# Norm2 between the first products of two pairs, two operand sets in the down-projection, and the gate row moved behind the sum

## Chip, cores and metric

The kernel runs on one core of one Trainium2 chip. The metric is the device time of one execution in microseconds (us), taken as the median of several runs.

## What is computed

One layer of a hybrid decoder, in float32: 1024 positions, model width 1024, and a gated MLP with 2816 channels in each half. The first sub-layer (attention and a state-space branch, with its output projection) is the first half of the kernel, and the change leaves it alone except for two buffers. What the change touches is the second sub-layer:

```python
h = _modulate(_rmsnorm(x, norm2_g[l]), sh2, sc2)          # norm2
up = _causal_dwconv(h @ ffn_w_up[l], ffn_conv_w[l], ffn_conv_b[l])
val, gate = jnp.split(up, 2, axis=-1)
x = x + g2[:, None, :] * ((jax.nn.gelu(gate) * val) @ ffn_w_down[l])
```

Here g2 is a row of 1024 gates, one for each output column. It is itself a product of the condition vector with a weight matrix, computed in the kernel.

## The kernel before

**Products.** Every float32 product is made of three matmuls of a reduced type: each operand is split into a high part (a copy, made on ScalarE, ACT) and a low part (a subtraction, made on VectorE, DVE), and hi·hi, hi·lo and lo·hi are summed in PSUM. A product of one 128-channel operand with a 512-deep, 512-wide block of the normalised input takes 12 such matmuls (lines 982 to 984).

**Up-projection.** The 2816 channels of each half are 22 pairs m of tiles (a value tile and its gate tile). For a pair the weights are a 2x2 block matrix A11, A12, A21, A22, and the normalised input is a 2x2 block matrix B11, B12, B21, B22; B11 and B21 come from the late half of the positions, the others from the early half. From pair 2 on the four block products of a pair are made by seven products in place of eight (Strassen-Winograd): the sums S1 to S4 of the weight blocks are made on GpSimd (POOL), and the sums T1 to T4 of the input blocks on DVE, once, in norm2. The seven products of a pair are A11·B11, A12·B21, S2·T2, S1·T1, S3·T3, S4·B22 and A22·T4. Pair 0 is made by eight products without S sums (A11, A12, A21, A22 with B11 and B21, then with T1, the early half's first block, and B22). Pair 1 is made by seven, with its first two products ahead. `up_raw` loads a weight block, `up_split` splits it, `up_early` does both, `up_operands` makes the operands of a pair with its sums, `product` issues the 12 matmuls, `conv` makes the convolution, the gelu and the gating of a pair and stores it to `a_d`.

**Norm2.** It is made by quarters g of the positions, in the order 3, 2, 1, 0. `norm2_x` scales the rows, `norm2_t` transposes them on TensorE (PE; `tp`, line 938), modulates them on ACT (`h2f`, line 939) and splits them. The quarters 3 and 2 give B11 and B21. The quarters 1 and 0 give T1 and B22, and `norm2_s` and `norm2_4` then give T2, T3 and T4: this is a chain of 128x512 operations that go back and forth between ACT and DVE.

**Down-projection.** The 1024 output columns are two halves n, the positions are eight tiles t, each with its own PSUM bank. `down_operands` loads 128 channels of the gated activations (`araw`) and of w_down (`wdraw`), multiplies the latter by the gate row g2row on POOL (line 1160), and splits both. `down` issues three matmuls for each t (lines 1174 to 1176). The last three m of each half are done tile by tile, and the tile's sum is added to the stored x (line 1189) and written out.

**What sets the order.** The program is written in the Tile framework. Its scheduler decides the order of instructions on each engine ahead of the run, from its own simulation; on the chip each engine takes its instructions strictly in that order. Buffers come from pools, and an instruction that reuses a buffer waits for the last reader. SyncE (SP) issues the loads and stores in order too: a transfer that has to wait for its buffer holds up all those behind it.

Of the kernel before, what the change touches and what calls it, by code (L numbers as in the profile page):

```python
# [9 lines left out]
F32 = mybir.dt.float32  # L10
F32R = mybir.dt.float32r
# [11 lines left out]
NT = 8  # L23
# [12 lines left out]
def hybrid_layer_kernel(  # L36
# [85 lines left out]

    A1 = const.tile([128, 8], F32, name="A1")
# [3 lines left out]
    g1row = const.tile([128, 1024], F32, name="g1row")  # L127
# [661 lines left out]
    def ssm_stats(inv):  # L789
        after_v(lambda: sp.dma_start(out=oS, in_=o_d.rearrange("(k p) j c -> p k j c", p=128)))  # L790
        yield
        yield from mix_scale(osp, psB_new("nps"), oS, range(NT), True, inv)
        yield
# [43 lines left out]
    def tail_stats(g):  # L837
        inv = small.tile([128, 2], F32, tag="ainv", name="ainv", bufs=4)
        run_all(mix_scale(osp, psB_new("nps"), oT, (2 * g, 2 * g + 1), False, inv))
        tail.append((g, inv))  # L840
        if len(tail) > 1 and g > 0:
            tail_proj()
# [51 lines left out]
    RAWS, OPS = 6, 7  # L894
# [117 lines left out]
    ups = [new_up() for _ in range(2)]  # L1012
    up = ups[0]
    a, b, c = new_bank(0, "a", "V", "a", 2), new_bank(0, "b", "V", "b"), new_bank(0, "c", "V", "a", 2)
    product(a, 0, "A11", B11, True, True)
    act_copy(up[0][:, LATE], a)
    product(b, 0, "A12", B21, True, True)
    tt(dve, up[0][:, LATE], b, up[0][:, LATE], ADD)
    product(c, 0, "A21", B11, True, True)
    act_copy(up[1][:, LATE], c)  # L1020
    d = new_bank(0, "d", "N", "b")
    product(d, 0, "A22", B21, True, True)
    tt(dve, up[1][:, LATE], d, up[1][:, LATE], ADD)
    product(new_bank(1, "a", "N", "c"), 1, "A11", B11, True)
    product(new_bank(1, "b", "V", "b"), 1, "A12", B21, True)

    norm2_t(1, norm2_x(1))
    norm2_s(1)
    with tc.high_priority():
        xn0 = norm2_x(0)  # L1030
# [5 lines left out]
    norm2_t(0, xn0)  # L1036
    psT.release()
    pools["D"] = alloc("psD", bufs=1, space=PSUM)
    product(a, 0, "A11", T1, False)
    product(c, 0, "A21", T1, False)  # L1040
    norm2_s(0)
    product(a, 0, "A12", B22, False)
    act_copy(up[0][:, EARL], a)
    product(c, 0, "A22", B22, False)
    act_copy(up[1][:, EARL], c)
    norm2_4(0)
    qp.release()
    uc = alloc("ffnconv", side="right")
    g2row = g1row
# [18 lines left out]
    def up_operands(m):  # L1068

        for r in range(2):  # L1070
            for c in range(2):
                if (m, r, c) not in raws:
                    up_raw(m, r, c)
        q11, q12, q21, q22 = [raws[m, r, c] for r in range(2) for c in range(2)]
        s1, s2, s3, s4 = [us.tile([128, 4, 128], F32, tag="S", name="S", bufs=4) for _ in range(4)]
        if m > 1:
            up_split(m, "A11", q11)
        tt(pool, s1, q21, q22, ADD)
        tt(pool, s2, s1, q11, SUB)
        if m > 1:  # L1080
            up_split(m, "A12", q12)
# [21 lines left out]
    def up_pair(m):  # L1103
        up_operands(m)
        up = ups[m] if m < 2 else new_up()
        if m > 1:
            a = new_bank(m, "a", "V", "a", 2)
            product(a, m, "A11", B11, True)
        a = bank[m, "a"]
        act_copy(up[0][:, LATE], a)  # L1110
        if m > 1:
            product(new_bank(m, "b", "NV"[m % 2], "b"), m, "A12", B21, True)
        b = bank[m, "b"]
# [14 lines left out]
    conv(0, ups[0])  # L1128
    for m in range(1, NM):
        up_pair(m)  # L1130
        if 6 <= m < 10:
            g2_rows(m - 6)
# [10 lines left out]
    us.release()  # L1143
    xq.release()
    da = alloc("dact")
    dw = alloc("dwgt")
# [3 lines left out]
    def down_operands(m, n):  # L1150
        raw = da.tile([128, 1024], F32, tag="araw", name="araw", bufs=2)
        sp.dma_start(out=raw, in_=a_d[m * 128:(m + 1) * 128, :])
        hi = da.tile([128, 1024], F32R, tag="ahi", name="ahi", bufs=4)
        lo = da.tile([128, 1024], F32R, tag="alo", name="alo", bufs=4)
        act_copy(hi, raw)
        tt(dve, lo, raw, hi.bitcast(F32), SUB)
        ns = slice(n * 512, (n + 1) * 512)
# [3 lines left out]
        whi = dw.tile([128, 512], F32R, tag="wdhi", name="wdhi", bufs=4)  # L1161
        wlo = dw.tile([128, 512], F32R, tag="wdlo", name="wdlo", bufs=4)
# [5 lines left out]
    for n in range(2):  # L1168
# [9 lines left out]
        for m in range(NM - TAIL):  # L1178
            ops = down_operands(m, n)
            for t in range(NT):  # L1180
                down(t, m, ops)
        ops = [down_operands(m, n) for m in range(NM - TAIL, NM)]
        for t in range(NT):
# [5 lines left out]
            tt(dve, res, o[t], res, ADD)  # L1189
# [4 lines left out]
    dw.release()  # L1194
    da.release()
# [63 lines left out]
```

## Time and profile before

| | us |
|---|---|
| median of 3 runs (1341.87 to 1342.91) | 1342.84 |
| the profiled execution | 1337.98 |
| its span in the trace | 1336.2 |
| TensorE busy in the span | 1211.5 (91%) |
| VectorE busy | 1019.7 (76%) |
| ScalarE busy | 594.0 (44%) |
| GpSimd busy | 535.4 (40%) |

All positions in time below are microseconds from the start of the span of this one profiled execution. The second sub-layer's matmuls begin at about 630 us, the down-projection at 1091 us. A bracket at the end of a row of a timeline gives the idle time of the engine ahead of the instruction and what ended it. "Clk" is the TensorE clock that was granted in a stretch, as a share of full speed.

### The profile page before, as it was taken

The page shows a single profiled execution, that of the slowest core. Times are in us where ns is not written, and L with a number is a line of the kernel's source. Part 1 is how long each engine was busy: PE and PEld are TensorE (multiplying, and loading weights), DVE is VectorE, ACT ScalarE, POOL GpSimd, SP SyncE. Part 2 cuts the span into 40 slices and gives each one's busy share as a digit, 9 for nine tenths or more (in the row PEclk, how much of TensorE's full clock was granted, in tenths as well). Part 3 has the DMA queues.
Part 4 walks back from the last instruction along what each step waited for, and adds up shares of the span by engine and source line. Part 5 has one row for each costly group of instructions (what it writes and reads, how often), then busy time and mean ns, then how long its engine had stood idle before and what let it go on. Part 6 is the DMA issues. An engine that isn't in the chain of part 4 may idle for free.

```text
span 1336.2 us, 16685 instructions
## 1 busy us (share of the span) xinstructions
PE 1211.5 (91%) x5740; PEld 989.2 (74%) x5740; DVE 1019.7 (76%) x1531; ACT 594.0 (44%) x1006; POOL 535.4 (40%) x415
## 2 busy tenths in 40 slices
PE   5879989999769988679788999999999989999998
PEld 4667768777557776568567888788888878888887
DVE  6999988973887999996799678877777666554552
ACT  5431333331565676535554554445554543222320
POOL 4472451431762446810253553454435334222330
PEclk9989979989679999889889999999999999999999
DMA  8462445557943755041024223322222145447543
GB/s 342 159 143 55 131 136 148 152 152 241 252 111 99 215 175 173 16 142 79 17 87 134 81 88 102 103 95 79 79 93 81 56 157 196 145 145 239 174 142 111
DMA packets 125632, 177.83 MB, mean 133 GB/s; under 512 B 36454, under 2 KB 73958, under 8 KB 124524
## 3 DMA queue, kind: packets, MB, share of 16 engines
q1 hardware_dynamic: 105484, 156.85, 37.7%
q10 hardware_dynamic: 20064, 19.93, 4.5%
q8 instruction: 45, 0.74, 0.2%
q14 instruction: 39, 0.32, 0.1%
HBM read 134.67 MB, written 40.89 MB: 131 GB/s over the span
## 4 chain that ended last, share of the span: by engine, by line
PE 54%; DVE 28%; DMA 8%; issue 4%; ACT 3%; POOL 1%; SPq 1%; DVEq 0%; ACTq 0%; POOLq 0%
PE dnps L1175 6%; PE dnps L1176 6%; PE dnps L1174 6%; PE up_a L982 5%; PE up_a L984 5%; PE up_a L983 5%; DVE ada_acc L67 4%; DVE nb L703 3%; DMA ada_raw<-in_ada_r_dram 3%; PE up_c L982 2%; PE up_c L984 2%; PE up_c L983 2%; PE wops L776 2%; PE wops L777 2%; PE wops L778 2%
## 5 line engine op out<-in xcount | busy, mean ns | idle before, releaser
L61 POOL TENSOR_TENSOR S<-upraw 128x512 f32<-128x512 f32 x42 | 83.4, 1987 | 253.3 <-DVE uplo L61 173.2
L1175 PE MATMUL dnps<-wdlo,ahi 128*128 128x512 f32 x352 | 137.2, 390 | 0.8 <-DVE wdlo L61 0.8
L1174 PE MATMUL dnps<-wdhi,ahi 128*128 128x512 f32 x352 | 134.6, 390 | 3.4 <-ACT wdhi L160 3.4
L1176 PE MATMUL dnps<-wdhi,alo 128*128 128x512 f32 x352 | 137.1, 390 | 0.0
L61 DVE TENSOR_TENSOR uplo<-S,uphi 128x512 fp32r<-128x512 f32 x84 | 96.4, 1151 | 45.4 <-ACT uphi L160 44.2
L61 DVE TENSOR_TENSOR alo<-araw,ahi 128x1024 fp32r<-128x1024 f32 x44 | 61.9, 1407 | 87.7 <-ACT ahi L160 87.7
L61 POOL TENSOR_TENSOR sig<-sig,nb 128x127 f32<-128x127 f32 (+3 forms) x64 | 94.2, 1479 | 84.2 <-DVE nb L703 58.2
L67 DVE SCALAR_TENSOR_TENSOR cv<-up,cols_sb,cv 128x1023 f32<-128x1023 f32 x88 | 116.2, 1322 | 14.3 <-ACT cv L1095 13.2
L61 POOL TENSOR_TENSOR wdraw<-wdraw,g1row 128x512 f32<-128x512 f32 x44 | 69.4, 1581 | 140.7 <-DMA wdraw<-in_w_down_dram 136.3
L703 DVE TENSOR_TENSOR_SCAN nb<-nb 128x128 f32<-128x128 f32 (+3 forms) x64 | 108.4, 1708 | 2.3 <-ACT nb L701 2.0
L160 ACT ACTIVATE ahi<-araw 128x1024 fp32r<-128x1024 f32 x44 | 46.6, 1060 | 141.8 <-PE dnps L1175 119.3
L160 ACT ACTIVATE uphi<-S 128x512 fp32r<-128x512 f32 x84 | 52.7, 631 | 103.6 <-PE up_c L983 30.9
L67 DVE SCALAR_TENSOR_TENSOR ada_acc<-ada_raw,c_sb,ada_acc 128x256 f32<-128x256 f32 (+1 forms) x97 | 73.4, 771 | 25.6 <-DMA ada_raw<-in_ada_r_dram 23.7
L553 PE MATMUL qkvp<-w_hi,hhi 128*128 128x512 f32 x192 | 78.8, 412 | 3.8 <-DVE qssq L606 2.9
L554 PE MATMUL qkvp<-w_lo,hhi 128*128 128x512 f32 x192 | 78.4, 408 | 0.8 <-POOL w_lo L61 0.8
L1174 PEld LDWEIGHTS dnps<-wdhi,ahi 128*128 128x128 f32 x352 | 66.0, 188 | 17.6 <-ACT wdhi L160 3.8
L555 PE MATMUL qkvp<-w_hi,hlo 128*128 128x512 f32 x192 | 77.4, 403 | 0.0
L1175 PEld LDWEIGHTS dnps<-wdlo,ahi 128*128 128x128 f32 x352 | 66.1, 188 | 14.9 <-DVE wdlo L61 1.2
L1176 PEld LDWEIGHTS dnps<-wdhi,alo 128*128 128x128 f32 x352 | 66.1, 188 | 13.5
L160 ACT ACTIVATE uphi<-upraw 128x512 fp32r<-128x512 f32 x67 | 41.8, 629 | 64.5 <-PE up_a L983 26.7
L61 POOL TENSOR_TENSOR cv<-cv 128x1024 f32<-128x1024 f32 x22 | 54.5, 2475 | 34.6 <-ACT cv L1099 34.5
L1095 ACT ACTIVATE cv<-up,cols_sb 128x1024 f32<-128x1024 f32 x44 | 54.7, 1244 | 24.5 <-DVE up L61 23.8
(328 smaller groups left out, 3515.5 us busy)
## 6 DMA issues: line engine op xcount, KB each, us to landing
upraw<-in_w_up_dram SPq DMA_DIRECT2D x88, 256.0 KB, 2.6
araw<-a_d SPq DMA_DIRECT2D x44, 512.0 KB, 3.3
ada_raw<-in_ada_r_dram SPq DMA_DIRECT2D x48, 256.0 KB, 3.1
a_d<-cv ACTq DMA_DIRECT2D x22, 512.0 KB, 2.7
wdraw<-in_w_down_dram SPq DMA_DIRECT2D x44, 256.0 KB, 3.3
ada_raw<-in_ada_a_dram SPq DMA_DIRECT2D x8, 1024.0 KB, 9.4
qk_d<-hl ACTq DMA_DIRECT2D x32, 256.0 KB, 3.0
q<-qk_d SPq DMA_DIRECT2D x32, 256.0 KB, 6.0
```

The lines of the kernel that those rows point to most:

```text
L61: eng.tensor_tensor(out=out, in0=a, in1=b, op=op)
L67: dve.scalar_tensor_tensor(out=out, in0=a, scalar=s, in1=b, op0=op0, op1=op1)
L160: act.activation(out=o, in_=i, func=AF.Copy)
L553: pe.matmul(o, lhsT=lh, rhs=his[k], start=(k == 0), stop=False)
L554: pe.matmul(o, lhsT=lh, rhs=los[k], start=False, stop=False)
L703: dve.tensor_tensor_scan(out=nb[:, 0:n][:, ::-1], data0=nb[:, 0:n][:, ::-1], data1=nb[:, 0:n][:, ::-1], initial=1.0, op0=MUL, op1=ALU.bypass)
L982: pe.matmul(ps, lhsT=hi[:, kt, :], rhs=rh, start=(first and kt == 0), stop=False, skip_group_check=True)
L983: pe.matmul(ps, lhsT=hi[:, kt, :], rhs=rl, start=False, stop=False, skip_group_check=True)
L984: pe.matmul(ps, lhsT=lo[:, kt, :], rhs=rh, start=False, stop=(kt == 3), skip_group_check=True)
L1174: pe.matmul(o[t], lhsT=hi[:, a], rhs=whi, start=(m == 0), stop=False)
L1175: pe.matmul(o[t], lhsT=hi[:, a], rhs=wlo, start=False, stop=False)
L1176: pe.matmul(o[t], lhsT=lo[:, a], rhs=whi, start=False, stop=(m == NM - 1))
```

## The change

Norm2's quarters 1 and 0 are moved between the first products of the pairs 0 and 1, and both pairs are made by eight products: pair 1's S sums go, and one product is added. The raw weight buffers are 4 and 2 in place of 6 common ones, the operand sets 8 in place of 7. The x tile's pool and the S pool stay allocated to the end, and the down-projection gets two separate sets of operand buffers, one of them in the room of B11 and B21. The multiplication by the gate row goes from w_down (POOL) to the finished sum (DVE, one more 128x512 operation for each of the 16 output tiles). The core of the diff:

```diff
@@ -891,13 +891,16 @@
-    RAWS, OPS = 6, 7
+    OPS, FIRST = 8, 2
...
-        raw = fu.tile([128, 4, 128], F32, tag="upraw", name="upraw", bufs=RAWS)
+        if m >= FIRST and r == 1:
+            raw = uc.tile([128, 4, 128], F32, tag="upraw", name="upraw", bufs=2)
+        else:
+            raw = fu.tile([128, 4, 128], F32, tag="upraw", name="upraw", bufs=4)
@@ -1009,23 +1012,36 @@
...
+    def first_late(m, pa, pb, pc, pd):
+        up = ups[m]
+        a = new_bank(m, "a", *pa)
+        product(a, m, "A11", B11, True, True)
+        act_copy(up[0][:, LATE], a)
+        b = new_bank(m, "b", *pb)
+        product(b, m, "A12", B21, True, True)
+        tt(dve, up[0][:, LATE], b, up[0][:, LATE], ADD)
...
+    def first_early(m):
+        up, a, c = ups[m], bank[m, "a"], bank[m, "c"]
+        product(a, m, "A11", T1, False)
+        product(c, m, "A21", T1, False)
+        product(a, m, "A12", B22, False)
+        act_copy(up[0][:, EARL], a)
+        product(c, m, "A22", B22, False)
+        act_copy(up[1][:, EARL], c)
 
     norm2_t(1, norm2_x(1))
+    first_late(0, ("V", "a", 2), ("V", "b"), ("V", "a", 2), ("N", "b"))
     norm2_s(1)
+    up_early(1, ("A21", "A22"))
     with tc.high_priority():
         xn0 = norm2_x(0)
@@ -1034,19 +1050,16 @@
     norm2_4(1)
     norm2_t(0, xn0)
+    first_late(1, ("N", "c"), ("V", "b"), ("N", "b"), ("V", "b"))
...
+    first_early(0)
     norm2_s(0)
...
+    first_early(1)
     norm2_4(0)
...
@@ -1140,26 +1149,23 @@
...
-    us.release()
-    xq.release()
-    da = alloc("dact")
-    dw = alloc("dwgt")
+
+    dps = [alloc(f"dops{i}") for i in range(2)]
...
-        raw = dw.tile([128, 512], F32, tag="wdraw", name="wdraw", bufs=3)
-        sp.dma_start(out=raw, in_=w_down[m * 128:(m + 1) * 128, ns])
-        tt(pool, raw, raw, g2row[:, ns], MUL)
...
+        raw = dp.tile([128, 512], F32, tag="wdraw", name="wdraw", bufs=2)
+        sp.dma_start(out=raw, in_=w_down[m * 128:(m + 1) * 128, n * 512:(n + 1) * 512])
...
+            with tc.high_priority() if (m, n) == (0, 0) else ExitStack():
+                ops = down_operands(m, n)
...
-            tt(dve, res, o[t], res, ADD)
+            t_ = dx.tile([128, 512], F32, tag="tmp", name="tmp", bufs=2)
+            tt(dve, t_, o[t], g2row[:, ns], MUL)
+            tt(dve, res, t_, res, ADD)
```

In SP's order, the loads of the first weight blocks (`upraw`) stood ahead of most of the stores of x (`x_d`). Before:

```order
L901 DMA upraw<-in_w_up_dram 128x512 x6
L852 DMA x_d<-xs 128x1024
L901 DMA upraw<-in_w_up_dram 128x512 x4
L852 DMA x_d<-xs 128x1024 x3
L852 DMA x_d<-xq_5302 128x1024 x2
L852 DMA x_d<-xq_5303 128x1024 x2
L901 DMA upraw<-in_w_up_dram 128x512 x2
```

The same place after the change:

```order
L852 DMA x_d<-xs 128x1024 x4
L904 DMA upraw<-in_w_up_dram 128x512 x6
L852 DMA x_d<-xq_5302 128x1024
L904 DMA upraw<-in_w_up_dram 128x512 x4
L852 DMA x_d<-xq_5302 128x1024
L904 DMA upraw<-in_w_up_dram 128x512 x2
L852 DMA x_d<-xq_5303 128x1024 x2
L904 DMA upraw<-in_w_up_dram 128x512 x2
```

The four stores from `xs` now stand ahead of all six loads, and the stores from `xq` stand between further loads.

On PE, the end of norm2, with the last transposes (`tp`) and the first products with T1 of pair 0 (up_a and up_c are the banks of a pair). Before:

```order
L938 MATMUL tp_6339<-ident,xn 128x128 x2
L938 MATMUL tp_6291<-ident,xn 128x128 x2
L938 MATMUL tp_6298<-ident,xn 128x128 x2
L938 MATMUL tp_6346<-ident,xn 128x128 x2
L938 MATMUL tp_6361<-ident,xn 128x128 x2
L938 MATMUL tp_6339<-ident,xn 128x128 x2
L938 MATMUL tp_6346<-ident,xn 128x128 x2
L938 MATMUL tp_6368<-ident,xn 128x128 x2
L938 MATMUL tp_6361<-ident,xn 128x128 x2
L938 MATMUL tp_6368<-ident,xn 128x128 x2
L982 MATMUL up_a<-T1hi_6158,uphi 128x512
L982 MATMUL up_c<-T1hi_6158,uphi 128x512
```

The same place after the change:

```order
L985 MATMUL up_d<-B21hi_5848,uphi 128x512
L986 MATMUL up_d<-B21lo_5850,uphi 128x512
L987 MATMUL up_d<-B21hi_5848,uplo 128x512
L985 MATMUL up_d<-B21hi_5848,uphi 128x512
L941 MATMUL tp_6347<-ident,xn 128x128 x2
L986 MATMUL up_d<-B21lo_5850,uphi 128x512
L987 MATMUL up_d<-B21hi_5848,uplo 128x512
L941 MATMUL tp_6354<-ident,xn 128x128 x2
L941 MATMUL tp_6347<-ident,xn 128x128 x2
L941 MATMUL tp_6354<-ident,xn 128x128 x2
L985 MATMUL up_a<-T1hi_6158,uphi 128x512
L985 MATMUL up_c<-T1hi_6158,uphi 128x512
```

Before, the last 22 transposes stood in a row behind the last product of the late half. Now the last of them stand between the matmuls of pair 1's product with B21 (up_d).

On ACT, the change from the up-projection to the down-projection (`ahi` and `wdhi` are the first operands of the latter, `cv` is the convolution). Before:

```order
L1095 ACTIVATE cv<-up,cols_sb 128x1024
L160 ACTIVATE up<-up_a 128x512
L1095 ACTIVATE cv<-up,cols_sb 128x1024
L160 ACTIVATE ahi<-araw 128x1024
L160 ACTIVATE wdhi<-wdraw 128x512
L1099 ACTIVATE cv<-cv 128x1024
L160 ACTIVATE ahi<-araw 128x1024
```

The same place after the change:

```order
L160 ACTIVATE up<-up_a 128x512
L1106 ACTIVATE cv<-up,cols_sb 128x1024
L160 ACTIVATE ahi<-araw 128x1024
L160 ACTIVATE up<-up_a 128x512
L160 ACTIVATE wdhi<-wdraw 128x512 x2
L160 ACTIVATE up<-up_a 128x512
L1106 ACTIVATE cv<-up,cols_sb 128x1024
L160 ACTIVATE ahi<-araw 128x1024
```

The first `ahi` and `wdhi` stood behind the last convolution of pair 21 (the second `cv<-up`, row before them); now they stand ahead of the evictions and the convolution of pair 21.

## Rows read from the trace of the kernel before

**Rows 1.** Page: busy us per engine; chain; a costly group; a DMA group.

```profile
PE 1211.5 (91%) x5740; PEld 989.2 (74%) x5740; DVE 1019.7 (76%) x1531; ACT 594.0 (44%) x1006; POOL 535.4 (40%) x415
...
PE 54%; DVE 28%; DMA 8%; issue 4%; ACT 3%; POOL 1%; SPq 1%; DVEq 0%; ACTq 0%; POOLq 0%
...
L61 POOL TENSOR_TENSOR wdraw<-wdraw,g1row 128x512 f32<-128x512 f32 x44 | 69.4, 1581 | 140.7 <-DMA wdraw<-in_w_down_dram 136.3
...
upraw<-in_w_up_dram SPq DMA_DIRECT2D x88, 256.0 KB, 2.6
```

**Rows 2.** Waits of PE, 630 to 700: us in total, times, longest.

```profile
PE tp L938 <- ACT h2f L939: 8.0, 5, 3.4
PE up_a L982 <- ACT uphi L160: 5.6, 1, 5.6
```

**Rows 3.** Stretches: length, then busy us (instructions) per engine, clk, DMA share, GB/s.

```profile
651.00:677.00 26.00, 12.15 (x36) 7.62 (x37) 22.85 (x37) 14.86 (x30) 13.54 (x3) 0.67 0.00 0
...
724.00:730.00 6.00, 5.93 (x19) 4.72 (x20) 4.37 (x9) 1.99 (x4) 1.40 (x1) 0.72 0.59 197
...
1100.00:1300.00 200.00, 200.00 (x884) 165.70 (x883) 107.04 (x86) 60.33 (x77) 62.50 (x39) 1.00 0.54 177
```

**Rows 4.** Timeline of PE, 646 to 666: start, duration, instruction, idle before.

```profile
646.75 0.82 PE L938 MATMUL tp<-ident,xn 128*128 128x128 f32 x6
647.33 0.47 PE L982 MATMUL up_b<-B21hi,uphi 128*128 128x512 f32 x1
...
665.16 0.63 PE L984 MATMUL up_a<-T1hi,uplo 128*128 128x512 f32 x1
665.58 0.63 PE L982 MATMUL up_a<-T1hi,uphi 128*128 128x512 f32 x1
```

**Rows 5.** Timeline of DVE, 640 to 676.

```profile
639.43 0.75 DVE L924 TENSOR_SCALAR xn<-xq,n2inv 128x1024 f32<-128x1024 f32 x1
...
648.04 0.69 DVE L61 TENSOR_TENSOR mix<-h2f,B11hi 128x512 f32<-128x512 f32 x1 [2.83 <-ACT h2f L939]
...
663.81 0.69 DVE L61 TENSOR_TENSOR T1lo<-mix,T1hi 128x512 fp32r<-128x512 f32 x1
...
669.83 0.70 DVE L61 TENSOR_TENSOR mix<-mix,B21lo 128x512 f32<-128x512 f32 x1
...
675.49 1.78 DVE L61 TENSOR_TENSOR T1lo<-mix,T1hi 128x512 fp32r<-128x512 f32 x1
```

**Rows 6.** Timeline of ACT, 672 to 676.

```profile
673.02 1.15 ACT L160 ACTIVATE uphi<-S 128x512 fp32r<-128x512 f32 x2 [6.97 <-POOL S L61]
674.08 0.62 ACT L160 ACTIVATE T1hi<-mix 128x512 fp32r<-128x512 f32 x1
```

**Rows 7.** Timeline of POOL, 640 to 676.

```profile
660.97 10.67 POOL L61 TENSOR_TENSOR S<-upraw 128x512 f32<-128x512 f32 x1 [79.98 <-DVE T L61]
671.72 1.26 POOL L61 TENSOR_TENSOR S<-S,upraw 128x512 f32<-128x512 f32 x1
```

**Rows 8.** Waits of PE, 700 to 800.

```profile
PE up_a L982 <- DVE up L61: 2.4, 2, 2.0
PE up_a L984 <- DVE uplo L61: 1.0, 1, 1.0
```

**Rows 9.** Timeline of SP, 587 to 640: the DMA issues.

```profile
593.35 14.23 SPq L852 DMA_DIRECT2D x_d<-xs  x3
```

**Rows 10.** Timeline of PE, 1090 to 1095: start of the down-projection.

```profile
1091.60 2.11 PE L1174 MATMUL dnps<-wdhi,ahi 128*128 128x512 f32 x8 [3.43 <-ACT wdhi L160]
1094.51 0.50 PE L1175 MATMUL dnps<-wdlo,ahi 128*128 128x512 f32 x1 [0.79 <-DVE wdlo L61]
```

**Rows 11.** Timeline of ACT, 1088 to 1092.

```profile
1089.99 1.04 ACT L160 ACTIVATE ahi<-araw 128x1024 fp32r<-128x1024 f32 x1
```

**Rows 12.** Timeline of DVE, 1330 to the end.

```profile
1332.39 0.69 DVE L61 TENSOR_TENSOR res<-dnps,res 128x512 f32<-128x512 f32 x1 [1.35 <-PE dnps L1176]
```

**Rows 13.** Waits of all engines, 730 to 1060.

```profile
POOL S L61 <- DVE uplo L61: 156.0, 32, 9.4
```

More of the change, by code (lines that the diff above doesn't have):

```diff
@@ L120, in hybrid_layer_kernel @@
     v_d = dram.tile([1024, 8, 128], F32, name="v_d")
+    g1row = const.tile([128, 1024], F32, name="g1row")
     A1 = const.tile([128, 8], F32, name="A1")
@@ L791, in ssm_stats @@
         yield
-        yield from mix_scale(osp, psB_new("nps"), oS, range(NT), True, inv)
+        yield from mix_scale(ap_, psB_new("nps"), oS, range(NT), True, inv)
         yield
@@ L1011, in hybrid_layer_kernel @@
     LATE, EARL = slice(512, 1024), slice(0, 512)
[L1012 to L1025, printed above, removed]
+    ups = [new_up() for _ in range(FIRST)]
+    def first_late(m, pa, pb, pc, pd):
[6 more added lines that the diff above has]
+        tt(dve, up[0][:, LATE], b, up[0][:, LATE], ADD)
+        c = new_bank(m, "c", *pc)
+        product(c, m, "A21", B11, True, True)
+        act_copy(up[1][:, LATE], c)
+        d = new_bank(m, "d", *pd)
+        product(d, m, "A22", B21, True, True)
+        tt(dve, up[1][:, LATE], d, up[1][:, LATE], ADD)
+    def first_early(m):
[6 more added lines that the diff above has]
+        act_copy(up[1][:, EARL], c)
     norm2_t(1, norm2_x(1))
+    first_late(0, ("V", "a", 2), ("V", "b"), ("V", "a", 2), ("N", "b"))
     norm2_s(1)
+    up_early(1, ("A21", "A22"))
     with tc.high_priority():
@@ L1036, in hybrid_layer_kernel @@
     norm2_t(0, xn0)
+    first_late(1, ("N", "c"), ("V", "b"), ("N", "b"), ("V", "b"))
     psT.release()
     pools["D"] = alloc("psD", bufs=1, space=PSUM)
-    product(a, 0, "A11", T1, False)
-    product(c, 0, "A21", T1, False)
+    first_early(0)
     norm2_s(0)
[L1042 to L1045, printed above, removed]
+    first_early(1)
     norm2_4(0)
     qp.release()
+    g2row = g1row
     uc = alloc("ffnconv", side="right")
-    g2row = g1row
     def g2_rows(q):
@@ L1104, in up_pair @@
         up_operands(m)
[L1105 to L1109, printed above, removed]
+        up = new_up()
+        a = new_bank(m, "a", "V", "a", 2)
+        product(a, m, "A11", B11, True)
         act_copy(up[0][:, LATE], a)
-        if m > 1:
-            product(new_bank(m, "b", "NV"[m % 2], "b"), m, "A12", B21, True)
-        b = bank[m, "b"]
+        b = new_bank(m, "b", "NV"[m % 2], "b")
+        product(b, m, "A12", B21, True)
         tt(dve, up[0][:, LATE], b, up[0][:, LATE], ADD)
@@ L1126, in up_pair @@
         conv(m, up)
-    conv(0, ups[0])
-    for m in range(1, NM):
+    for m in range(FIRST):
+        conv(m, ups[m])
+    for m in range(FIRST, NM):
         up_pair(m)
@@ L1150, in down_operands @@
     def down_operands(m, n):
[L1151 removed]
+        dp = dps[m % 2]
+        raw = dp.tile([128, 1024], F32, tag="araw", name="araw", bufs=1)
         sp.dma_start(out=raw, in_=a_d[m * 128:(m + 1) * 128, :])
[L1153 to L1154 removed]
+        hi = dp.tile([128, 1024], F32R, tag="ahi", name="ahi", bufs=2)
+        lo = dp.tile([128, 1024], F32R, tag="alo", name="alo", bufs=2)
         act_copy(hi, raw)
         tt(dve, lo, raw, hi.bitcast(F32), SUB)
[L1157 to L1162 removed]
+        raw = dp.tile([128, 512], F32, tag="wdraw", name="wdraw", bufs=2)
+        sp.dma_start(out=raw, in_=w_down[m * 128:(m + 1) * 128, n * 512:(n + 1) * 512])
+        whi = dp.tile([128, 512], F32R, tag="wdhi", name="wdhi", bufs=2)
+        wlo = dp.tile([128, 512], F32R, tag="wdlo", name="wdlo", bufs=2)
         act_copy(whi, raw)
@@ L1193, in hybrid_layer_kernel @@
     dx.release()
-    dw.release()
-    da.release()
+    for dp in reversed(dps):
+        dp.release()
+    us.release()
+    xq.release()
     small.release()
```

10 lines of the change are left out of this document (3 added, 7 removed).

## Prediction

> **What bounds the kernel now.** I read the page first: TensorE (PE) is busy for 1211.5 of 1336.2 us and makes up 54% of the chain that ended last, VectorE (DVE) 28% [rows 1]. The down-projection is at its limit: from 1100 to 1300 PE is busy for 200.00 of 200 us with 884 matmuls, 0.226 us each, at the full granted clock [rows 3]. A change to the feeding engines earns nothing there. So I looked, in the waits of PE and by stretches, for the places in the second half of the kernel where PE is not full. There are three.
>
> First, norm2. Between 630 and 700 us PE waits 8.0 us for the modulated tiles of ScalarE (ACT) and once 5.6 us for a split on ACT [rows 2]. In the 26 us from 651 to 677 it runs 36 instructions [rows 3]: 20 matmuls, 4.5 us at 0.226, and 16 transposes, 1.6 us at 0.097 (six take 647.33 - 646.75 [rows 4]). So 26 - 6.1 = **19.9 us** are lost. Part of that is the clock: it is 0.67 on average in this stretch [rows 3], and matmuls stand 0.42 us apart instead of 0.226 [rows 4], which is the 1.2 GHz level after the idle times. What holds PE up is DVE: from 648.04 to 669.83 it works through a row of 38 operations of 0.60 us without a gap (the first and the last are [rows 5]; the count is 22.4 / 0.60). The first low part of T1 of quarter 0 is its 27th (663.81), the second comes at 675.49 [rows 5], because its high part stands on ACT behind a split of an S sum, and ACT waits 6.97 us for that sum [rows 6].
>
> Second, from 700 to 800 us PE waits 2.4 + 1.0 us for DVE [rows 8], and behind the longest of these waits it runs 19 instructions in 5.93 us [rows 3], 1.6 us more than at 0.226: **5.0 us** in all.
>
> Third, the start of the down-projection: 3.43 us of waiting for `wdhi`, and 0.79 us for `wdlo` [rows 10]: **4.2 us**. ACT took the first `ahi` only at 1089.99, behind the convolution of the last pair [rows 11].
>
> **The change, part by part.**
>
> *Norm2's quarters between the first products.* PE's order shows that the transposes of quarter 1 now follow 13 matmuls of pair 0, where 72 stood before them. They can't come 59 x 0.226 = 13.3 us earlier, because their input `xn` is made by DVE at 639.43 + 0.75 [rows 5]; DVE's row then starts at about 641.8 instead of 648.04, some 6.2 us earlier (an estimate: transposes and one ACT operation behind `xn`). It has 34 operations up to the first T1 low part of quarter 0, since the additions of two pairs now stand among them, against 26 before: 641.8 + 34 x 0.60 = 662.3. So DVE itself wins 1.5 us there only. The gain comes from PE's side: the late products of both pairs, 96 matmuls, and 34 transposes fill the time: 632.5 (where PE turns to them) + 21.7 + 3.3 = 657.5. It then waits until 660 to 662, where T1's high and low parts come: I take **3.9 us** of loss. Behind that 96 matmuls of the early products have their operands before they need them: T1's second low part comes at about 666.6, as no split of an S sum stands ahead of its high part on ACT any more. The price is one more product, 12 x 0.226 = **2.7 us**. Sum: -19.9 + 3.9 + 2.7 = **-13.3 us**. Bounds: -17.2 if PE doesn't wait at all; if DVE's row is 6 us later than I count, -7.
>
> *The first loads.* The loads of pair 0 go behind four stores from `xs`, of which the last three are issued from 593.35 to 607.58 [rows 9]. A load then lands 2.6 us later [rows 1] and the six at about 611 to 613, while PE wants the operands at 632. The splits fall among ACT's and DVE's work of the output projection; before, they were done earlier. Bounds 0 and +3; I take **+1**.
>
> *The stretch behind norm2.* Pair 1's four sums go from POOL, and its S splits from ACT and DVE, but the convolutions of two pairs and the gate row's sums still meet there. I keep half of the 5.0 us, by the margins of about 1 us that I count for DVE's splits: **-2.5**, bounds -5.0 and +2.
>
> *Two operand sets.* The first `ahi` and `wdhi` move ahead of the last pair's evictions and convolution on ACT, and their buffers no longer wait for anything that ends late: they take the room of B11 and B21. What is queued behind them on ACT is an eviction of the last pair; it comes 1 to 1.6 us later, with products of 2.7 us between them. For m=1 the margin of `wdlo` is 0.8 us or more by my count. **-4.2**, bounds -4.2 and 0.
>
> *The multiplication by the gate row.* 44 operations of 1.58 us go from POOL [rows 1], none on the path, as PE is full there [rows 3]. In their place stand 16 on DVE; a tile's last operation takes 0.69 us and DVE was idle for 1.35 us ahead of it [rows 12], so that seven of the last eight hide. The last one doesn't: **+0.7**, bounds 0.6 and 1.4.
>
> *Buffers of the weights in the steady state.* The load of A22 of a pair now waits for the split of A22 of the pair before. Behind it stand the load (2.6 us [rows 1]), two sums, a split on ACT and one on DVE, before PE needs S2. By order I count about 18 matmuls, 4 us, of slack in each pair, and POOL has time: in 17 pairs it waited 156.0 us for DVE's splits [rows 13]. I take 0.
>
> Sum: -13.3 + 1 - 2.5 - 4.2 + 0.7 = -18.3 us. The span goes from 1336.2 to 1317.9, the profiled execution of 1337.98 to 1319.7. The median is 4.9 us above that execution, and I give the forecast against the median: 1342.8 - 18.3 = **1324.5**. All the better ends give -25.8 (1317), all the worse -0.6 (1342).
>
> **A rule weighed.** In the trace a sum of two SBUF tiles on POOL took 10.67 us at 660.97, beside DVE's unbroken row, and the next one, when DVE paused, 1.26 us [rows 7]. The Trainium skill's "SBUF — State Buffer", section "Who interferes with whom", says that a DVE instruction with two SBUF inputs and a GpSimd instruction that reads SBUF keep each other out; the trace agrees for this row.
>
> **Rivals.**
>
> *DVE's row stays the bound.* The chain between ACT and DVE comes later than I count, with more of the additions ahead of it, and PE cools down while it waits. For it: DVE wins only 1.5 us at the first T1; each later operation costs 0.60. Against it: PE has 96 matmuls more to wait with. At 6 us later, and with the stretch behind it unchanged, 1342.8 - (7 + 0 + 4.2 - 1.7) = **1333**.
>
> *POOL is shut out.* The sums of pair 2 meet DVE's row as the one at 660.97 did, are 9.4 us late (10.67 - 1.26), and PE reaches S2 of pair 2 some 24 matmuls (5.4 us) after its own start; with about 4 us of slack PE stands for 5 us: 1324.5 + 5 = **1330**. For it: the row. Against it: by then DVE's row is through, at about 671.
>
> *The loads of A21 and A22 starve PE in the steady state.* This ends on the slower side. Two buffers instead of a common six make a loop through load, POOL, ACT, DVE and PE in every pair. If it is longer by d than the slack of 4 us, PE loses d in each of some 19 pairs. From d = 0.96 us the whole gain of 18.3 is gone; at d = 2 the time is 1324.5 + 38 = **1362**. For it: sums on POOL took up to 10.67 us [rows 7], and SP's queue is in order. Against it: POOL's idle time [rows 13].
>
> *Only the start of the down-projection comes out.* The time in norm2 goes into the added product, the late loads and a wait behind norm2: 1342.8 - 4.2 + 0.7 = **1339**.
>
> **How the numbers follow.** Forecast 0.58, DVE bound 0.18, POOL shut out 0.08, starving 0.09, only the start 0.07. The forecast's own range is 1319 to 1330; taking in the second and the third gives **1317 to 1336**, which leaves the last two out. A measurement of this kernel can tell about 0.2% (2.7 us) from no change: faster means under 1340.1, slower over 1345.5. Slower has most of the starving case, 0.08; same 0.04; faster 0.88.
>
> **What would show it.** Right: PE's waits for `tp` of 8.0 us and for `uphi` of 5.6 us are gone, PE waits once, at T1, for under 5 us; from the first T1 matmul on some 96 run without a break; no wait above 1 us at the first matmul of the down-projection; two DVE operations behind the last matmul. Wrong: idle time of PE in every pair from 730 to 1060, ended by a split of S (starving); the matmuls of the late products broken by waits for `uphi` at 632 (loads); a sum on POOL of about 10 us ahead of pair 2 (shut out); PE at the clock of 0.67 again beyond 660 (DVE bound).

## Result and profile after

The changed kernel takes 1327.68 us (median, 1325.94 to 1332.28) where the kernel before takes 1342.36: a ratio of 0.9899 with a 95% interval of 0.9871 to 0.9926, 14.7 us less by the medians. Run again beside later experiments it gave 1329.41 against 1342.33, a ratio of 0.9905 (0.9890 to 0.9921), 12.9 us less. The forecast was 1324.5, 18.3 us less.

The profiled execution has a span of 1324.6 us, 11.6 us under the 1336.2 of before. Of the page after, the busy time and share of each engine, answering to [rows 1]:

```profile
PE 1213.3 (92%) x5752; PEld 992.6 (75%) x5752; DVE 1010.3 (76%) x1543; ACT 587.1 (44%) x1003; POOL 467.5 (35%) x367
```

TensorE (PE) has 12 more instructions, one product; GpSimd (POOL) has lost 68 us of work.

To say where the time went I summed, for both traces, PE's lost time: the distance between the starts of successive PE instructions that goes beyond 0.2266 us for each matmul of 512 columns and 0.097 us for each transpose. It holds waits and slow clock together.

| PE's lost time (us) | before | after | after, again |
|---|---|---|---|
| norm2, 640 to 680 us | 20.4 | 6.1 | 6.9 |
| 680 to 740 us | 6.2 | 1.0 | 1.5 |
| 780 to 860 us | 2.2 | 10.3 | 10.2 |
| start of the down-projection, 1080 to 1100 us | 4.8 | 0.0 | 0.0 |

So norm2 gave more or less what was forecast, and a new loss of 8 us stands where the forecast had none.

**Norm2.** PE's waits from 632 to 700 us after the change (us in total, times, longest), answering to [rows 2]:

```profile
PE up_a L986 <- DVE T1lo L61: 1.4, 1, 1.4
PE tp L941 <- ACT h2f L942: 0.9, 1, 0.9
PE up_a L985 <- ACT T1hi L160: 0.7, 1, 0.7
```

Before, these were 8.0 us for `h2f` and 5.6 us for a split of an S sum. The stretch 651 to 677 of [rows 3] now has 100 PE instructions instead of 36, at a mean clock of 0.93 instead of 0.67 (columns: stretch, length, busy us and instructions of PE, PEld, DVE, ACT, POOL, then clock, DMA share, GB/s):

```profile
651.00:677.00 26.00, 23.04 (x100) 17.96 (x99) 25.13 (x40) 15.90 (x29) 2.56 (x2) 0.93 0.10 31
```

In the timeline of PE after the change, what is left of the loss can be read line by line, answering to [rows 4]:

```profile
659.86 0.90 PE L941 MATMUL tp<-ident,xn 128*128 128x128 f32 x4 [0.87 <-ACT h2f L942]
661.47 0.50 PE L985 MATMUL up_a<-T1hi,uphi 128*128 128x512 f32 x1 [0.71 <-ACT T1hi L160]
...
664.02 0.50 PE L986 MATMUL up_a<-T1lo,uphi 128*128 128x512 f32 x1 [1.35 <-DVE T1lo L61]
...
664.66 0.63 PE L985 MATMUL up_a<-T1hi,uphi 128*128 128x512 f32 x1
665.09 0.63 PE L986 MATMUL up_a<-T1lo,uphi 128*128 128x512 f32 x1
```

Three waits add up to 2.9 us. Behind the last one, matmuls stand 0.43 us apart until 667.65, the level of 1.2 GHz: seven of them, 1.4 us more. Then PE runs without a wait to 700 us.

VectorE (DVE) shows why PE still waits there, answering to [rows 5]:

```profile
643.22 0.69 DVE L61 TENSOR_TENSOR mix<-h2f,B11hi 128x512 f32<-128x512 f32 x1 [2.23 <-ACT h2f L942]
...
663.28 0.68 DVE L61 TENSOR_TENSOR T1lo<-mix,T1hi 128x512 fp32r<-128x512 f32 x1
...
667.49 0.68 DVE L61 TENSOR_TENSOR T1lo<-mix,T1hi 128x512 fp32r<-128x512 f32 x1
```

The row of DVE starts 4.8 us earlier than before, and T1's first low part is made 0.5 us earlier than before only (663.81); but PE has done 24 more late matmuls by then. The second low part is 8 us earlier (before: 675.49), because no split of an S sum stands ahead of its high part.

**The new loss.** All engines' waits from 780 to 860 us after the change; first what ScalarE (ACT), GpSimd and VectorE waited for, then PE:

```profile
ACT uphi L160 <- POOL S L61: 16.2, 3, 7.3
POOL S L61 <- DMA upraw<-in_w_up_dram: 13.8, 2, 8.5
POOL S L61 <- DVE g2acc L67: 10.5, 1, 10.5
DVE g2acc L67 <- DMA g2raw<-in_ada_r_dram: 8.8, 6, 3.0
...
PE adps L1078 <- DVE g2acc L67: 2.6, 1, 2.6
...
PE up_a L985 <- ACT up L160: 2.3, 2, 1.4
...
PE up_c L985 <- ACT up L160: 1.3, 1, 1.3
PE up_a L985 <- DVE up L61: 0.9, 1, 0.9
```

In the kernel before, POOL's long waits in the same stretch were for DVE's splits (43.9 us, the longest 9.4, and PE didn't feel them). Now it waits for weight loads. Such waits alone cost PE nothing: in the kernel without the gate row (below), in which PE is full in this stretch, the same row reads

```profile
POOL S L61 <- DMA upraw<-in_w_up_dram: 13.6, 3, 4.5
```

One chain in which the wait reaches PE, after the change, in the timelines of SyncE (SP), VectorE (DVE), POOL, ACT and PE:

```profile
805.66 4.81 SPq L1072 DMA_DIRECT2D g2raw<-in_ada_r_dram  x4
811.34 0.33 SPq L904 DMA_DIRECT2D upraw<-in_w_up_dram  x1
```

```profile
809.11 1.01 DVE L67 SCALAR_TENSOR_TENSOR g2acc<-g2raw,c_sb,g2acc 128x256 f32<-128x256 f32 x2 [2.96 <-DMA g2raw<-in_ada_r_dram]
...
810.63 0.68 DVE L61 TENSOR_TENSOR uplo<-upraw,uphi 128x512 fp32r<-128x512 f32 x1
```

```profile
814.01 2.38 POOL L61 TENSOR_TENSOR S<-upraw 128x512 f32<-128x512 f32 x1 [8.53 <-DMA upraw<-in_w_up_dram]
```

```profile
818.64 1.15 ACT L160 ACTIVATE uphi<-S 128x512 fp32r<-128x512 f32 x2 [4.04 <-POOL S L61]
819.70 0.58 ACT L160 ACTIVATE up<-up_c 128x512 f32<-128x512 f32 x1
```

```profile
820.33 0.50 PE L985 MATMUL up_c<-B22hi,uphi 128*128 128x512 f32 x1 [1.28 <-ACT up L160]
```

Four blocks of the gate row are issued, each waiting for one of two buffers. DVE waits 2.96 us for one of them to land, and behind its sums the split `uplo<-upraw` is queued; it ends at 811.31. The weight block behind the four is issued at 811.34: SP had come to it 0.8 us earlier, and what it waited for was this split, which frees its buffer.

```profile
SPq L904 <- DVE uplo L61: 0.8, 1, 0.8
```

POOL's sum waits for the block 8.53 us; ACT stands at the split of that sum 4.04 us, and the eviction `up<-up_c` is queued behind it; PE needs the bank, and waits 1.28 us for the eviction. So the weight load is late because DVE stands at a gate block, and not because gate loads stand ahead of it on SP. It is the same elsewhere in this stretch: the first weight load behind each group of gate loads is issued as soon as a split on DVE or a sum on POOL has freed its buffer (except two behind single gate loads, at 839.03 and 840.99).

Four waits of PE for evictions, and the time lost just behind them, make 5.9 of the 10.3 us. The other 4.4 us lie at one place, where PE's own product of the gate row waits for its sum and the matmuls behind it run at the 1.2 GHz level:

```profile
845.71 1.22 PE L1078 MATMUL adps<-g2acc,ones 128*128 128x256 f32 x2 [2.55 <-DVE g2acc L67]
...
847.16 0.63 PE L986 MATMUL up_a<-B11lo,uphi 128*128 128x512 f32 x1
847.58 0.63 PE L987 MATMUL up_a<-B11hi,uplo 128*128 128x512 f32 x1
```

**Start and end of the down-projection.** No wait of PE over the stretch 1060 to 1110 is left (before: 3.43 and 0.79 us [rows 10]). At the end two operations of DVE stand where [rows 12] had one, 0.73 us apart (`g1row` is the tile whose room the gate row g2row takes):

```profile
1320.08 0.69 DVE L61 TENSOR_TENSOR tmp<-dnps,g1row 128x512 f32<-128x512 f32 x1 [0.62 <-PE dnps L1182]
1320.81 0.69 DVE L61 TENSOR_TENSOR res<-tmp,res 128x512 f32<-128x512 f32 x1
```

One thing belongs to the reading of all the times here. TensorE's instructions up to some 590 us stand in the same order in these kernels, yet the last matmul of the output projection stands at 633.34 us before, at 633.35 after, and between 630.37 and 638.44 us in the profiles of the experiments. A single span is therefore good to some 4 us either way. The comparisons below rest on ratios of many runs, and on PE's lost time by stretch, which doesn't contain the first half.

### The profile page after: what moved, and what is told of

Same layout as the page of the kernel before. It is cut to its first block, busy times and chain, and to the rows that moved or that the text cites. A ratio compares the mean times of both kernels' runs of the same rounds, so it can differ in the third digit from the quotient of the medians.

```text
span 1324.6 us, 16659 instructions
## 1 busy us (share of the span) xinstructions
PE 1213.3 (92%) x5752; PEld 992.6 (75%) x5752; DVE 1010.3 (76%) x1543; ACT 587.1 (44%) x1003; POOL 467.5 (35%) x367
## 4 chain that ended last, share of the span: by engine, by line
PE 58%; DVE 25%; DMA 7%; issue 5%; ACT 3%; POOL 2%; SPq 1%; DVEq 0%; ACTq 0%; POOLq 0%
PE dnps L1181 6%; PE dnps L1180 6%; PE dnps L1182 6%; PE up_a L986 5%; PE up_a L985 5%; PE up_a L987 5%; DVE ada_acc L67 3%; DMA ada_raw<-in_ada_r_dram 3%; DVE nb L703 3%; PE up_c L986 2%; PE up_c L987 2%; PE up_c L985 2%; PE wops L776 2%; DVE cv L67 2%; PE wops L778 2%
## 5 line engine op out<-in xcount | busy, mean ns | idle before, releaser
L67 DVE SCALAR_TENSOR_TENSOR cv<-up,cols_sb,cv 128x1023 f32<-128x1023 f32 (+1 forms) x88 | 136.6, 1554 | 16.6 <-ACT cv L1106 15.9
L61 POOL TENSOR_TENSOR S<-upraw 128x512 f32<-128x512 f32 x40 | 72.8, 1820 | 208.0 <-DMA upraw<-in_w_up_dram 144.7
L61 DVE TENSOR_TENSOR alo<-araw,ahi 128x1024 fp32r<-128x1024 f32 x44 | 53.9, 1224 | 120.2 <-ACT ahi L160 120.1
L61 DVE TENSOR_TENSOR uplo<-S,uphi 128x512 fp32r<-128x512 f32 x80 | 90.7, 1140 | 19.8 <-ACT uphi L160 19.4
L160 ACT ACTIVATE uphi<-S 128x512 fp32r<-128x512 f32 x80 | 49.1, 625 | 89.5 <-POOL S L61 69.4
L710 PE MATMUL wT<-ident,sig 128*128 128x128 f32 x288 | 50.4, 302 | 14.1 <-POOL sig L61 8.7
L714 ACT ACTIVATE wh<-wT 128x512 fp32r<-128x512 f32 (+2 forms) x96 | 45.4, 497 | 37.6 <-PE wT L710 24.2
```

The costliest lines, as they stand in the source:

```text
L61: eng.tensor_tensor(out=out, in0=a, in1=b, op=op)
L67: dve.scalar_tensor_tensor(out=out, in0=a, scalar=s, in1=b, op0=op0, op1=op1)
L160: act.activation(out=o, in_=i, func=AF.Copy)
```

## Experiments

**The two halves of the change apart.** The first has the changed kernel's norm2 and products, and the down-projection of before:

```diff
-    dps = [alloc(f"dops{i}") for i in range(2)]
+    us.release()
+    xq.release()
+    da = alloc("dact")
+    dw = alloc("dwgt")
...
+        tt(pool, raw, raw, g2row[:, ns], MUL)
...
-            tt(dve, t_, o[t], g2row[:, ns], MUL)
-            tt(dve, res, t_, res, ADD)
+            tt(dve, res, o[t], res, ADD)
```

> The changed kernel with the down-projection of before: one set of operand buffers, the gate row multiplied into w_down on GpSimd, one addition at the end. Up to the first operand of the down-projection its order of instructions on TensorE and SyncE is that of the changed kernel. If the two halves of the change add up, as the traces of before and after say (TensorE's lost time from 620 to 1080 us goes from 29.2 to 17.7 us, one product of 2.7 us is added), it takes about 8.8 us less than before, 1333.5, with waits of 3.4 and 0.8 us at the first matmuls of the down-projection. If the down-projection's buffers or the missing GpSimd multiplications pay for more than the 4.2 us at its start, it lies above 1336.

Measured: 1335.13 against 1340.14, ratio 0.9953 (0.9933 to 0.9973), 6.3 us less by the ratio and not 8.8. PE's lost time agrees with the changed kernel up to 860 us (6.9 in norm2, 9.7 from 780 to 860), but at the start of the down-projection it is 7.9 us, more than the 4.8 of before. PE's waits there:

```profile
PE dnps L1184 <- ACT wdhi L160: 3.4, 1, 3.4
PE dnps L1185 <- DVE wdlo L61: 1.3, 1, 1.3
```

Most of the rest of the 7.9 us is the clock, which fell behind these waits: from the timeline of PE,

```profile
1092.98 0.63 PE L1186 MATMUL dnps<-wdhi,alo 128*128 128x512 f32 x1
1093.40 0.62 PE L1185 MATMUL dnps<-wdlo,ahi 128*128 128x512 f32 x1
```

0.42 us apart, as [rows 4] at 665 us. So norm2's part alone is worth about 8.1 us up to the down-projection in the traces, of which 3.1 are lost again there.

The second is the kernel before with the new down-projection; its diff is the first one turned round, on the code of before.

> The kernel before with only the down-projection of the changed one: two operand sets, the gate row behind the sum. Up to the end of the up-projection its order on TensorE is that of before. If the gain is the 4.2 us of waiting at the start of the down-projection, less one operation of 0.7 us at the end: 1342.4 - 3.5 = 1338.9, no wait over 0.5 us at the first matmuls. If the first operands, taken early, push evictions of the last pair back on ScalarE, it lies at 1342 or above.

Measured: 1337.24 against 1340.14, ratio 0.9974 (0.9956 to 0.9991), 3.5 us less by the ratio. No wait of PE at the first matmuls is left, and its lost time there is 0.4 us instead of 4.8. This is what the forecast's 4.2 - 0.7 gives, within the interval. The two halves (6.3 + 3.5 = 9.8) don't quite add up to the whole (13 to 14), because the new down-projection also takes away the 7.9 us that the first half has there alone, where it takes 4.4 from the kernel before.

**Is the eighth product the cover, or the order of the transposes?** Pair 1 was made by seven products again, its first two ahead, and the transposes left among the first products:

```diff
-    first_late(1, ("N", "c"), ("V", "b"), ("N", "b"), ("V", "b"))
+    product(new_bank(1, "a", "N", "c"), 1, "A11", B11, True)
+    product(new_bank(1, "b", "V", "b"), 1, "A12", B21, True)
...
-    first_early(1)
...
-    for m in range(FIRST, NM):
+    for m in range(1, NM):
```

> The changed kernel with pair 1 made by seven products, its first two ahead as in the kernel before; norm2's transposes still stand among the first products. If the eighth product is the cover that fills TensorE's time in norm2, 24 matmuls (5.4 us) less of cover and the S sums back on GpSimd beside VectorE's row cost more than the 2.7 us of the product that is saved: 3 to 8 us above the changed kernel, 1331 to 1336, with a wait for the split of an S sum again near 665 us. If the order of the transposes alone made the gain, it takes 2.7 us less than the changed kernel, 1325.

Measured: 1340.06, ratio 0.9996 (0.9978 to 1.0014): no gain over the kernel before is left, and it lies some 13 us above the changed kernel, more than I expected. PE's lost time in norm2 is 15.8 us against 6.1, and its waits from 632 to 700 us are

```profile
PE up_a L985 <- ACT uphi L160: 4.0, 1, 4.0
PE tp L941 <- ACT h2f L942: 3.5, 1, 3.5
PE up_a L986 <- DVE T1lo L61: 0.5, 1, 0.5
```

The wait for a split of an S sum is back. Eight products for pair 1 cost 2.7 us more than seven and save 9.7 in norm2; the order of the transposes alone takes only 4.6 of the 20.4 us away. Whether the 9.7 us are the added matmuls or the missing S sums of pair 1 this run doesn't tell apart, since the eight products bring both; the waits speak for each in about equal parts. Another 5 us were lost from 780 to 880 us (15.4), the same place as in the changed kernel; PE waited there mostly for DVE, and why is not settled.

**What is lost from 780 to 860 us?** First the gate row's computation was left out altogether:

```diff
-        if 6 <= m < 10:
-            g2_rows(m - 6)
```

> The changed kernel without the computation of the gate row of the second half (its loads, its sums on VectorE and its four products are left out). In the changed kernel TensorE loses 10.3 us from 780 to 860 us, where the row's loads stand among the weight loads on SyncE's queue; before it lost 2.2 us there. If these loads hold up the weight loads of A21 and A22, which have only two buffers, that loss goes: about 9 us less than the changed kernel, 1318.5. If the two buffers starve TensorE by themselves, waits for evictions and sums remain in 730 to 1060 us, and it lies within 2 us of the changed kernel.

Measured: 1315.58 against 1340.14, ratio 0.9809 (0.9781 to 0.9837), 25.6 us under the kernel before, some 12 under the changed kernel. The stretches 780 to 860 and 860 to 1060 of this kernel:

```profile
780.00:860.00 80.00, 80.00 (x354) 66.24 (x354) 68.87 (x59) 40.62 (x60) 42.87 (x21) 1.00 0.23 82
860.00:1060.00 200.00, 200.00 (x884) 165.58 (x884) 169.43 (x146) 101.29 (x145) 101.83 (x50) 1.00 0.23 80
```

PE is full. The two buffers for the weight blocks don't starve it by themselves; the gate row does it. In the kernel before, though, the gate row stood at the same pairs and cost at most 2.2 us there, so it takes something of the change besides. By the chain above this is the two buffers, since a weight block is now issued only when a split or a sum of the pair before has freed one (before, no wait of POOL in this stretch was for a weight load). No run gave these loads their six buffers back, so that is argued and not shown.

Of the gate row it can be the loads or the sums, so next the sums stayed, and 28 of the 32 loads were left out (each sum reads one block eight times):

```diff
-            raw = uc.tile([128, 256], F32, tag="g2raw", name="g2raw", bufs=2)
-            sp.dma_start(out=raw, in_=ada_r[ix, :, r, o:o + 256])
             if r == 0:
+                raw = uc.tile([128, 256], F32, tag="g2raw", name="g2raw", bufs=2)
+                sp.dma_start(out=raw, in_=ada_r[ix, :, r, o:o + 256])
```

> The changed kernel with the gate row's sums unchanged in number, but made from one loaded block for each quarter in place of eight (28 of 32 loads are left out, so the gate row has other values). The sums on VectorE, its 32 operations, and the products stay. If the loads on SyncE's queue, which wait for two buffers and hold up the weight loads behind them, cause the loss of 10.3 us from 780 to 860 us, it goes down to about that of the kernel without the gate row: 8 to 10 us less than the changed kernel, about 1318 where the kernel before takes 1341. If VectorE's added operations cause it, the time stays within 2 us of the changed kernel, 1327.

Measured: 1323.02 against 1342.97, ratio 0.9851 (0.9821 to 0.9882). In time this is 5 to 7 us less than the changed kernel, and not the 8 to 10 that I expected. PE's lost time from 780 to 860 us is 3.0 instead of 10.3 us, and in this stretch

```profile
780.00:860.00 80.00, 78.13 (x342) 63.48 (x341) 70.57 (x83) 36.09 (x55) 36.22 (x20) 1.00 0.23 80
```

PE has 342 instructions, where the changed kernel had 310. DVE is even busier (70.57 us; it was 65.22), so it isn't the amount of DVE's work that PE waits for. What is gone are DVE's waits for gate blocks (8.8 us in the changed kernel) and PE's wait for the product of the gate row. Without the 28 loads 7.3 of the 10.3 us are gone. The traffic as such doesn't do it: by the pages of the two profiles, a weight block takes a median of 3.1 us from issue to landing in the changed kernel and 3.0 in the one without the gate row.

Do the loads do it by standing in SP's queue? They were given to ACT's queue, and, in another run, to POOL's:

```diff
-            sp.dma_start(out=raw, in_=ada_r[ix, :, r, o:o + 256])
+            act.dma_start(out=raw, in_=ada_r[ix, :, r, o:o + 256])
```

> The changed kernel with the gate row's 32 loads issued by ScalarE in place of SyncE. If the weight loads are late because they stand behind gate loads that wait for their two buffers, the weight loads are free now and most of the loss of 10.3 us from 780 to 860 us goes: 5 to 8 us less than the changed kernel, unless ScalarE itself now stands at these loads and its evictions come late, which would show as waits of TensorE for evictions and no gain. If the traffic itself (not the queue) makes the weight loads late, no gain either, but with the sums on GpSimd waiting for the loads.

> The changed kernel with the gate row's 32 loads issued by GpSimd. GpSimd was idle for more than half of the stretch, so if SyncE's queue is the cause, 5 to 8 us less than the changed kernel; if GpSimd's issuing or its waiting for the two buffers delays the S sums, the loss stays or grows, and the waits of ScalarE for S sums show it.

Measured beside the changed kernel again (ratio 0.9905): ACT's queue 1328.98, ratio 0.9895 (0.9874 to 0.9916); POOL's queue 1332.71, ratio 0.9938 (0.9921 to 0.9955). Neither takes the 5 to 8 us less that I expected if SP's queue was the cause: the first equals the changed kernel within the interval, the second lies some 4 us above it. On ACT's queue the loss from 780 to 880 us falls to 6.5 us, but 2 us more are lost ahead of 700 us; on POOL's queue 10.7 us are lost from 760 to 880, and 4.6 from 700 to 720. The waits of the version on ACT's queue show ACT standing at the loads (from 780 to 860 us):

```profile
POOL S L61 <- DMA upraw<-in_w_up_dram: 15.5, 2, 8.1
...
ACT uphi L160 <- DVE g2acc L67: 9.9, 4, 4.4
```

ACT's split stands behind a gate load that waits for `g2acc` to free its buffer. POOL's sums wait for weight blocks as long as before, although no gate load stands on SP any more. What the weight loads wait for on SP in this version are the readers of their own buffers:

```profile
SPq L904 <- DVE uplo L61: 38.9, 5, 10.4
SPq L904 <- POOL S L61: 24.7, 4, 8.6
```

This agrees with the chain above: standing in SP's queue is not what makes the weight loads late. What moving the loads to ACT took away is PE's wait for the product of the gate row; of the 5.9 us at the evictions nothing clear is gone. An engine that issues the gate loads stands at them itself (ACT for 9.9 us here, POOL for 14.1 us in its version), so these two runs don't test SP's queue alone. How the 7.3 us divide among DVE's waits for the blocks, PE's product and SP's queue is read from the traces, and no run separates them.

The changed kernel itself was run again beside these:

> The changed kernel once more, unaltered, beside the next three on the same chip. Both theories: about 13.5 us less than the kernel before, with TensorE losing some 10 us from 780 to 860 us and some 6 us from 640 to 680 us again, if these losses belong to the order of instructions and not to one execution.

Its losses are those of the table: 6.9 and 10.2 us. They belong to the order of the program.

**Can the loss be spread?** The gate row is needed only at the end now, so its quarters can stand further apart:

```diff
-        if 6 <= m < 10:
-            g2_rows(m - 6)
+        if m in (8, 11, 14, 17):
+            g2_rows((m - 8) // 3)
```

> The changed kernel with the gate row's four quarters behind the pairs 8, 11, 14 and 17 in place of 6, 7, 8 and 9; the number of loads and operations is the same. If it is the crowding of four quarters within some 70 us that lets the slack of the pairs run out, most of the loss of 10.3 us goes, since the pairs between recover: 5 to 9 us less than the changed kernel, 1319 to 1322. If each quarter costs by itself, by its loads ahead of a pair's weight loads, the loss stays at about 2.5 us for each: 1327.

> The changed kernel with the gate row's quarters behind the pairs 5, 9, 13 and 17 and three buffers for its blocks in place of two, so that a load waits less for VectorE's sums. If SyncE's queue standing at a gate block is what holds up the weight loads, it gains on the version with two buffers and quarters three pairs apart: 7 to 10 us less than the changed kernel, 1317 to 1320. If the buffers don't matter, it equals that version.

> The gate row's quarters behind the pairs 8, 11, 14 and 17, and its loads issued by ScalarE. If queue and crowding are both part of the loss, it is the fastest of these: 8 to 10 us less than the changed kernel. If spreading alone gave what there is to gain, it equals the version with spread quarters on SyncE, 2 to 4 us less than the changed kernel.

Measured: spread 1325.94, ratio 0.9873 (0.9845 to 0.9901); quarters behind 5, 9, 13 and 17 with three buffers 1329.43, 0.9893 (0.9862 to 0.9924); spread and on ACT's queue 1325.77, 0.9881 (0.9863 to 0.9899). PE's lost time beyond 780 us is 6.8 us for the first, 14.0 for the second and 5.7 for the third (of it 1.0 at the start of the down-projection), against 10.3. Spreading takes back some 4 us in the traces, less than the 5 to 9 that I expected of it, and the times of the two versions with two buffers lie 2 to 4 us under the changed kernel; the intervals overlap, so that they beat it is likely and not shown. Against what I expected of it, the version with a third buffer did worse: three of its quarters cost 3.9 to 5.9 us each. Whether that is the buffer or the other pairs isn't settled. Each quarter goes on costing something, so crowding is part of the cause and not the whole of it.

**Is GpSimd's multiplication off the path?** The changed kernel with the gate row multiplied into w_down again:

```diff
+        tt(pool, raw, raw, g2row[:, n * 512:(n + 1) * 512], MUL)
...
-            tt(dve, t_, o[t], g2row[:, ns], MUL)
-            tt(dve, res, t_, res, ADD)
+            tt(dve, res, o[t], res, ADD)
```

> The changed kernel with the gate row multiplied into w_down on GpSimd again (44 operations of 1.58 us) and one addition for each output tile. If these operations are off the path and the second operation at the end costs 0.7 us, it takes 0.7 us less than the changed kernel, which is within the noise: 1326 to 1327. If GpSimd in the chain from load to first operand brings a wait back at the start of the down-projection, or slows the splits on VectorE so that TensorE waits, it takes 2 us or more above the changed kernel.

Measured: 1332.42 against 1342.97, ratio 0.9925 (0.9900 to 0.9950): some 3 us above the changed kernel by the ratios, whose intervals overlap. In the trace the wait is back, on the third m:

```profile
1092.16 2.06 PE L1181 MATMUL dnps<-wdhi,ahi 128*128 128x512 f32 x6 [3.12 <-ACT wdhi L160]
```

Its cause is DVE: the four convolution operations of the last pair, in this kernel and then in the changed one,

```profile
1082.43 8.01 DVE L67 SCALAR_TENSOR_TENSOR cv<-up,cols_sb,cv 128x1023 f32<-128x1023 f32 x4 [1.31 <-ACT cv L1106]
```

```profile
1080.08 5.16 DVE L67 SCALAR_TENSOR_TENSOR cv<-up,cols_sb,cv 128x1023 f32<-128x1023 f32 x4 [1.38 <-ACT cv L1106]
```

take 8.01 us beside POOL's multiplications and 5.16 us without them. Three of the four overlap an operation of POOL and take 2.20 to 2.33 us; the last takes 1.28 us, as each does in the changed kernel. ACT's gelu waits for them, and `wdhi` is queued behind the gelu.

## Why the prediction came out as it did

The direction and the range held; the gain was 13 to 15 us and not 18.3. By the forecast's steps, with the trace's numbers:

| step | forecast | measured |
|---|---|---|
| norm2, with the added product | -13.3 | -20.4 + 6.1 + 2.7 = -11.6 |
| first loads | +1 | no wait of PE for them |
| the stretch behind norm2 | -2.5 | -6.2 + 1.0 = -5.2 |
| weight buffers in the steady state | 0 | -2.2 + 10.3 = +8.1 |
| start of the down-projection | -4.2 | -4.8 |
| gate row behind the sum | +0.7 | +0.7 |
| sum | -18.3 | -12.8 |

The miss of 8.1 us in one row was partly made up by the stretch behind norm2 (2.7 us better) and the first loads (1 us), which the forecast hadn't counted on: that much is luck.

**The step that failed is the steady state, "I take 0".** It measured +8.1 us. The count of slack held for pairs without the gate row: from 860 to 1060 us PE is full, in the changed kernel as in the one without the gate row. It left out the pairs in which DVE also makes the gate row's sums and stands at their blocks. The third rival's loop through load, POOL, ACT, DVE and PE did open there, in those pairs instead of 19, and made 5.9 of the 10.3 us (2.3 us near 790 to 797, 3.5 near 820 to 826). What the rival had for it, SP's order, was not what made the loop too long; DVE's was. The other 4.4 us, PE's wait for the product of the gate row, stood in no term and no rival. That the two buffers are needed for the loss is argued from the chain. The evidence against the rival, POOL's idle time of [rows 13], said nothing, since POOL's idle time is where such a wait shows. What I should have asked is what frees the buffer of each weight load, and what that engine has to wait for ahead of it.

**Norm2 was right in mechanism and a little small in its loss**: 6.1 us instead of 3.9. The waits come to 2.9 us, less than I took; the rest is slow clock behind them (1.4 us), for which the sum had no term, and small gaps. The time of T1's first low part was counted as 662.3, the trace has 663.28; the second 666.6 and 667.49. DVE's row started at 643.22 and not at 641.8 as estimated, and this low part was its 33rd operation where 34 were counted (the row before the change has 37 operations, not 38; no term hangs on it). That making pair 1 by eight products, and not the earlier transposes, makes most of the gain was the argument, and making pair 1 by seven showed it; that it is the added matmuls rather than the missing S sums is not shown.

**The stretch behind norm2** came out better than the half I kept of it: the loss of 6.2 us (I had counted 5.0) went almost wholly. So the rival in which POOL is shut out didn't take place either. Pair 2's first sum ran when DVE's row was through and took 1.58 us, not 10.67 as in [rows 7]:

```profile
674.36 1.58 POOL L61 TENSOR_TENSOR S<-upraw 128x512 f32<-128x512 f32 x1 [90.63 <-DMA upraw<-in_w_up_dram]
```

**At the start of the down-projection** the size was right, and its reasons were incomplete. The forecast gave the gain to the two operand sets and nothing to the missing multiplications ("none on the path"). For the kernel before that was so: POOL's multiplications were done ahead of the last convolution, whose four operations took no longer than after the change,

```profile
1087.57 5.15 DVE L67 SCALAR_TENSOR_TENSOR cv<-up,cols_sb,cv 128x1023 f32<-128x1023 f32 x4 [1.38 <-ACT cv L1095]
```

But with the new operand sets and the multiplications kept, the two meet, and 5.2 us are lost there again: POOL slows DVE's convolution, 2.00 us for each operation on average instead of 1.29. This is the rule that the prediction weighed, from the Trainium skill's "SBUF — State Buffer", section "Who interferes with whom": DVE operations with two SBUF inputs and a GpSimd instruction that reads SBUF keep each other out. The two rows of the experiment agree with it.

## What to carry to other kernels

Where an engine waits in a chain that other engines set, one product more than needed can be worth several times its price, if it gives that engine work and takes work from the others; the transposes in another order, without it, took away only a quarter of the loss here. When buffers of a steady loop are split up or made fewer, count the loop's slack in the pass with the most other work, and ask for each load which engine frees its buffer: here a small load that landed late held up an engine, and with it the buffer of the next large load. Nor is an operation free because its engine has idle time: look at what the others do beside it, at the places where the bound engine waits.

## What the runs showed of the hardware

With the same order of TensorE's instructions up to 590 us, the end of the output projection lay between 630.37 and 638.44 us, a spread of 8 us from the first half alone. A wait of 1.35 us at 664.02 us, behind shorter ones, was followed by seven matmuls at the 1.2 GHz level; a wait of 3.12 us at 1092.16 us in the kernel with the multiplications kept was part of a loss of 5.2 us. Four convolution operations of VectorE took 8.01 us beside GpSimd's multiplications and 5.16 us without: the three that overlapped an operation of GpSimd took 2.20 to 2.33 us, all others 1.28 to 1.29. A weight load took 3.1 us to land with the gate row's loads beside it and 3.0 us without them.
